# Down projection of an MLP as seven block products on one Trainium2 core, with the sums of weights on GpSimd

## The chip, the core and the metric

The kernel runs on one core of a Trainium2 chip. The core has TensorE (PE, matrix products into PSUM), VectorE (DVE), ScalarE (ACT), GpSimd (POOL) and SyncE (SP, which issues most DMAs). The metric is the time of one execution on the device in microseconds (us), as a median over runs.

## The reference

Two blocks follow one another on x of 512 positions by 1024 channels: a recurrent layer and an attention layer, then two hybrid layers. The change is in the MLP at the end of each hybrid layer:

```
h2 = rmsnorm(x, norm_mlp)
return x + jnp.square(jax.nn.relu(h2 @ w_up)) @ w_down     # w_up 1024x4096, w_down 4096x1024
...
for i in range(DEPTH):                                       # DEPTH = 2
    x = hybrid_layer(x, ...)
return rmsnorm(x, norm_final)
```

Everything is float32. On the chip each operand of a product is split into a high part (rounded to the matmul's input type) and a low part (the rest), and every product is three matmuls: high by high, high by low, low by high.

## The kernel before

**Layout.** Channels lie on the 128 partitions and positions on the free axis, so x is 8 tiles of 128x512. Weights come from HBM in chunks of 128x1024 (512 KB), each of which gives one output tile of 128 channels: 8 steps over the input channels, three matmuls each (`mm3`, L261 to L264).

**Stream of weights.** `Stream` loads the chunks in a fixed list `items` and splits each one: ACT writes the high part (L60), DVE subtracts to get the low part (L61). `next()` hands out one and emits the following one or two, so the weights of a pair are split while the pair before it is multiplied. Four raw buffers, three for high and three for low parts, and three for the split sums limit how far this runs ahead.

**MLP.** The 4096 hidden channels go in four groups of 1024 (`g`). In each group the up projection makes 8 hidden tiles, then the down projection adds their part to the 8 tiles of x. Up is done in *pairs* of output tiles by a Strassen-Winograd scheme: two output tiles by two halves of the positions are a 2x2 block product over two halves of the input channels, done in 7 block products instead of 8. Each block product is 4 steps of three matmuls with 256 columns, so 84 matmuls a pair. It needs sums of weight blocks S1 to S4 (`_emit_sums`, L63: two chunks come in, four adds of 128x512 on one engine, then two splits of 128x1024 and three of 128x512) and sums of x (T1 to T4, made once a layer by `PairNorm`). `W.pooled = 4` puts the adds of the first four pairs of a layer on POOL, the others on DVE. Each product has a PSUM bank of its own, and ACT, DVE and POOL combine the seven (L403 to L414). The hidden tile is then scaled by the row `r`, clipped at zero, squared and split (L1156, L1157, L277, L278).

**Down** is plain: per output tile 8 steps of three matmuls with 512 columns (192 matmuls in a group), then one DVE add into x (L1175). The last group of the last layer does three of its tiles by halves of the positions in `finish`, which also does the final norm and the output.

**Order.** PE's order is that of the code. On the other engines a scheduler orders the instructions at build time; each engine then runs its own list in that order and waits on semaphores, so whatever stands behind a waiting instruction waits too.

Of the kernel before, what the change touches and what calls it, by code (L numbers as in the profile page):

```python
# [7 lines left out]
F32 = mybir.dt.float32  # L8
# [40 lines left out]
class Stream:  # L49


    def __init__(self, tc, raw, hi, lo, items, ahead):
        self.nc, self.raw, self.hi, self.lo = tc.nc, raw, hi, lo
        self.items, self.ahead = items, ahead
        self.done, self.taken = [], 0
        self.sums = self.sraw = None
        self.pooled = 0
# [5 lines left out]
    def _emit_sums(self, i, s1, s2):  # L63
# [5 lines left out]
        eng = nc.gpsimd if self.pooled > 0 else nc.vector  # L69
        self.pooled -= 1  # L70
# [15 lines left out]
        def half(nm, src):  # L86
            h = self.sums.tile([P, nh], F32R, tag="shi", name=f"sh{i}{nm}")
            l = self.sums.tile([P, nh], F32R, tag="slo", name=f"sl{i}{nm}")
            self._split(h, l, src)
            out[nm] = tuple(t.rearrange("p (a b) -> p a b", b=P) for t in (h, l))  # L90
# [18 lines left out]
    def _emit(self):  # L109
        nc = self.nc  # L110
        src, a, b = self.items[len(self.done)]
        if a is None:
            return self._emit_sums(len(self.done), src, b)
# [19 lines left out]
    def next(self):  # L133
        ahead = 1 if self.items[self.taken][1] is None else self.ahead
        self.prefetch(self.taken + 1 + ahead)
        out = self.done[self.taken]
        self.done[self.taken] = None
        self.taken += 1
        return out

# [12 lines left out]
def build(tc, A, out, dbg=None):  # L153
# [3 lines left out]
    with ctx:  # L157
# [50 lines left out]
        for l in range(2):  # L208
# [21 lines left out]
            for g in range(4):  # L230
                for f in range(0, 8, 2):
                    items.append((A[f"w_up{l}"][8 * g + f], None, A[f"w_up{l}"][8 * g + f + 1]))
                for j in range(8):
                    add(f"w_down{l}", 8 * g + j, KD, P)
# [19 lines left out]
        xH = big.tile([P, KD, S], F32R, name="xH")  # L254
        xL = big.tile([P, KD, S], F32R, name="xL")
# [5 lines left out]
        def mm3(ps, wH, wL, aH, aL, start, stop):  # L261
            pe.matmul(ps, wH, aH, start=start, stop=False)  # L262
            pe.matmul(ps, wH, aL, start=False, stop=False)  # L263
            pe.matmul(ps, wL, aH, start=False, stop=stop)  # L264

        def proj(ps, wch, srcH=None, srcL=None, mid={}):
            h, l = wch
            srcH = xH if srcH is None else srcH
            srcL = xL if srcL is None else srcL
            for k in range(KD):  # L270
                mm3(ps, h[:, k], l[:, k], srcH[:, k], srcL[:, k], k == 0, k == KD - 1)
# [33 lines left out]
        class Norm:  # L305
# [8 lines left out]
            def split(self, j):  # L314
                g = self.gain[:, j:j + 1]
                act.activation(xH[:, j], x[:, j], AF.Copy, scale=g)
                self.last = dve.scalar_tensor_tensor(xL[:, j], x[:, j], g, xH[:, j].bitcast(F32), ALU.mult, ALU.subtract).ins
# [28 lines left out]
        class PairNorm:  # L346


            def __init__(self, tag, tp, gain, TH, TL):
                self.n = Norm(tag, tp)  # L350
                self.gain, self.TH, self.TL, self.tp, self.tag = gain, TH, TL, tp, tag
                self.rows = self.n.rows

            def tile(self, j):
                self.n.tile(j)
                if j < 4:
# [4 lines left out]
                    split(xH[:, j, :S2], xL[:, j, :S2], xa[:, :S2])  # L361
# [10 lines left out]
                split(xH[:, j], xL[:, j], xb)  # L372
                split(self.TH[:, k, 2:], self.TL[:, k, 2:], d[:, 2:])

        def pair(tag, forms, cp, cs, first=False):
# [3 lines left out]
            ps = {}  # L379

            def prod(n, wn, xn, ks=range(4), stop=True):
                if n not in ps:
                    ps[n] = psum(f"{tag}_{n}")[:, :S2]
                h, l = w[wn]
                for k in ks:
                    bh, bl = forms[xn](k)
                    mm3(ps[n], h[:, k], l[:, k], bh, bl, k == 0, stop and k == 3)

            steps = ((1, "A11", "B11"), (2, "A12", "B21"), (5, "S1", "T1"), (6, "S2", "T2"))
            if first:  # L390
                for st in steps:
                    prod(*st, range(3), False)
                for st in steps:
                    prod(*st, range(3, 4))
            else:
                for st in steps:
                    prod(*st)
            s1 = cs.tile([P, S2], F32, tag="s1", name=f"s1_{tag}")
            s5 = cs.tile([P, S2], F32, tag="s5", name=f"s5_{tag}")
            z = cs.tile([P, S2], F32, tag="sz", name=f"sz_{tag}")  # L400
            c1 = cp.tile([P, S], F32, tag="c", name=f"c1_{tag}")
            c2 = cp.tile([P, S], F32, tag="c", name=f"c2_{tag}")
            act.copy(s1, ps[1])  # L403
            dve.tensor_add(c1[:, :S2], ps[2], s1)
            act.copy(s5, ps[5])
            dve.tensor_add(z, ps[6], s1)  # L406
            pool.tensor_add(s5, s5, z)  # L407
            prod(7, "S3", "T3")
            dve.tensor_add(z, ps[7], z)
            dve.tensor_add(c2[:, S2:], ps[7], s5)  # L410
            prod(3, "S4", "B22")
            dve.tensor_add(c1[:, S2:], ps[3], s5)
            prod(4, "A22", "T4")
            dve.tensor_add(c2[:, :S2], ps[4], z)  # L414
            return c1, c2

        def x_forms(TH, TL):
            S2 = S // 2
            f = {f"T{i + 1}": (lambda k, i=i: (TH[:, k, i], TL[:, k, i])) for i in range(4)}
            f["B11"] = lambda k: (xH[:, k, :S2], xL[:, k, :S2])  # L420
            f["B21"] = lambda k: (xH[:, 4 + k, :S2], xL[:, 4 + k, :S2])
            f["B22"] = lambda k: (xH[:, 4 + k, S2:], xL[:, 4 + k, S2:])
# [209 lines left out]
        with ExitStack() as lc:  # L632
# [58 lines left out]
            def fox_v(c, mid=None):  # L691
# [4 lines left out]
                for tb in range(4):  # L696
                    ps = psum(f"v{c}_{tb}")[:, :n]
                    cs = slice(tb * P, (tb + 1) * P)
                    for k in range(KD):
                        h, l = w[k // kt]  # L700
                        mm3(ps, xH[:, k, cs], xL[:, k, cs], h[:, k % kt], l[:, k % kt], k == 0, k == KD - 1)
# [167 lines left out]
        def finish(ah, nrm, tp):  # L869

            S2, JS = S // 2, (5, 6, 7)
            ws = [W.next() for _ in JS]
            onesf = ones.bitcast(F32)
            for j in range(3, 5):
# [3 lines left out]
            def down(b, j, mid):  # L878
                h, l = ws[j - JS[0]]
                hs = slice(b * S2, (b + 1) * S2)  # L880
                ps = psum(f"dl{j}_{b}")[:, :S2]
                for k in range(8):
                    mm3(ps, h[:, k], l[:, k], ah[k][0][:, hs], ah[k][1][:, hs], k == 0, k == 7)
                    if k in mid:
                        mid[k]()
# [3 lines left out]
                if j == 7:  # L889
# [11 lines left out]
            def norm(b):  # L901
# [4 lines left out]
                for i, j in enumerate((3, 0, 1, 2, 4, 5, 6, 7)):  # L906
                    o = os[j // 4][:, j % 4 * S2:j % 4 * S2 + S2]
                    if j in (3, 4):
# [9 lines left out]

            none = {}
            down(0, 5, none)  # L920
            down(0, 6, none)
            down(0, 7, none)
            down(1, 5, {3: lambda: (sum_start(0), sum_end(0), norm(0))})
            down(1, 6, none)
            down(1, 7, none)
# [4 lines left out]
        for li in range(2):  # L930
# [3 lines left out]
            with ExitStack() as lc:  # L934
# [71 lines left out]
                for h in range(RET_H):  # L1006
# [13 lines left out]
                    for tb in range(4):  # L1020
                        ps = psum(f"rv{li}_{h}_{tb}")[:, :256]
                        cs = slice(tb * P, (tb + 1) * P)
                        for k in range(KD):
                            wh, wl = (h0, l0) if k < 4 else (h1, l1)
                            mm3(ps, xH[:, k, cs], xL[:, k, cs], wh[:, k % 4], wl[:, k % 4], k == 0, k == KD - 1)
# [56 lines left out]
            with ExitStack() as lc:  # L1082
# [50 lines left out]
                W.pooled = 4  # L1133
# [6 lines left out]
            with ExitStack() as lc:  # L1140
                t1 = lc.enter_context(tc.tile_pool(name=f"u{li}_1", bufs=1))
                t2 = lc.enter_context(tc.tile_pool(name=f"u{li}_2", bufs=2))
                t4 = lc.enter_context(tc.tile_pool(name=f"u{li}_4", bufs=4))
                ta = lc.enter_context(tc.tile_pool(name=f"u{li}_a", bufs=8))
                forms = x_forms(TH, TL)
                tn = Map(cs_h=(ta, "aH"), cs_l=(ta, "aL"), rs_m=(t4, "c"), rs_t=(t4, "c"), nsq=(t4, "c"))
                for g in range(4):
                    ah = []
                    for f in range(0, 8, 2):
                        cc = pair(f"up{li}_{g}_{f}", forms, t4, t2, g == 0 and f == 0)  # L1150
                        if g == 0 and f == 0:
                            r = nrm.rows(tn)
                            nrm = Norm(f"x{li}", tn, None if last else v("nmix1", 0, 8))
                        for i in range(2):
                            t = cc[i]
                            dve.scalar_tensor_tensor(t, t, 0.0, r, ALU.max, ALU.mult)  # L1156
                            act.activation(t, t, AF.Square)  # L1157
                            aH = ta.tile([P, S], F32R, tag="aH", name=f"aH{li}_{g}_{f + i}")
                            aL = ta.tile([P, S], F32R, tag="aL", name=f"aL{li}_{g}_{f + i}")
                            split(aH, aL, t)  # L1160
                            ah.append((aH, aL))
                    head = [(W.next(), psum(f"dn{li}_{g}_{j}")) for j in range(2)]
                    for ks in (range(6), range(6, 8)):
                        for (h, l), ps in head:
                            for k in ks:
                                mm3(ps, h[:, k], l[:, k], ah[k][0], ah[k][1], k == 0, k == 7)
                    for j in range(5 if last and g == 3 else 8):
                        if j < 2:
                            ps = head[j][1]
                        else:  # L1170
                            h, l = W.next()
                            ps = psum(f"dn{li}_{g}_{j}")
                            for k in range(8):
                                mm3(ps, h[:, k], l[:, k], ah[k][0], ah[k][1], k == 0, k == 7)
# [113 lines left out]
```

## Time and profile before

| | |
|---|---|
| median of 3 runs | 2275.84 us (2275.23 to 2277.53) |
| the profiled execution | 2277.16 us, of which the span from first to last instruction is 2275.1 us |
| PE busy | 98% of the span |
| DVE, ACT, POOL busy | 68%, 47%, 16% |
| granted TensorE clock, mean | 0.989 of full speed |

The profiled execution lies 1.3 us above the median. An engine counts as busy also while an instruction that it has begun is held up inside the engine, so a busy share is no measure of work done. DVE pipelines: the next instruction begins about 0.08 us before the one ahead of it ends, so the step from start to start is what an instruction costs.

### The profile page before, as it was taken

Reading aid. Unit: us, or ns where it says so; the run is one execution under the profiler, and the core shown is the slowest. Engines: PE = TensorE matmul, PEld = TensorE weight load, DVE = VectorE, ACT = ScalarE, POOL = GpSimd, SP = SyncE. Lnnn points to the kernel's source line nnn. Section 1 sums busy time; section 2 is a strip of 40 time slices with the busy share of each in tenths; the row PEclk is TensorE's granted clock in tenths of the full one; section 3 lists DMA queues with packets and bytes.
Section 4 is the critical chain, followed back from the end, with each engine's and each line's share of the span. In section 5 each row is a group of like instructions: output and inputs, shape, how many; then the busy total and the mean of one; then the engine's idle time right before and its main releaser. Section 6 shows DMA issues by size and latency. Waiting matters only on the chain.

```text
span 2275.1 us, 30068 instructions
## 1 busy us (share of the span) xinstructions
PE 2220.2 (98%) x11818; PEld 1912.8 (84%) x11818; DVE 1543.0 (68%) x2256; ACT 1066.3 (47%) x1629; POOL 372.7 (16%) x269
## 2 busy tenths in 40 slices
PE   8899999999999999999999999999999999999998
PEld 6687778887888888887998998988888887998997
DVE  8988877777776445448876785676345448886774
ACT  5666577765555222235543444556222235543443
POOL 3435211113211000003310112211000003310112
PEclk9999999999999999999999999999999999999999
DMA  4123222122232322222332333222332232333231
GB/s 155 64 95 102 90 66 75 65 74 81 71 105 75 100 95 95 100 93 84 104 101 95 110 103 102 90 92 74 102 102 93 97 98 76 110 103 101 96 110 56
DMA packets 62509, 210.42 MB, mean 92 GB/s; under 512 B 6944, under 2 KB 11424, under 8 KB 62368
## 3 DMA queue, kind: packets, MB, share of 16 engines
q1 hardware_dynamic: 59552, 204.43, 27.2%
q10 hardware_dynamic: 2672, 3.81, 0.5%
q8 instruction: 93, 1.52, 0.3%
q14 instruction: 48, 0.39, 0.1%
q0 software_dynamic: 144, 0.26, 0.0%
HBM read 206.37 MB, written 2.10 MB: 92 GB/s over the span
## 4 chain that ended last, share of the span: by engine, by line
PE 83%; DVE 4%; ACT 1%; issue 1%; POOL 0%; DVEq 0%; ACTq 0%; POOLq 0%
PE dn L263 5%; PE dn L262 5%; PE dn L264 5%; PE up L263 5%; PE up L264 5%; PE up L262 5%; PE ro L987 1%; PE gb L262 1%; PE cu L263 1%; PE cc L263 1%; PE cb L263 1%; PE wr L263 1%; PE gb L263 1%; PE gb L264 1%; PE wc L262 1%
## 5 line engine op out<-in xcount | busy, mean ns | idle before, releaser
L60 ACT CAST wh<-wr 128x1024 fp32r<-128x1024 f32 (+2 forms) x332 | 337.5, 1018 | 691.0 <-PE dn L263 110.1
L61 DVE TENSOR_TENSOR wl<-wr,wh 128x1024 fp32r<-128x1024 f32 (+2 forms) x332 | 401.0, 1209 | 49.4 <-ACT wh L60 47.2
L263 PE MATMUL dn<-aL,wh 128*128 128x512 f32 x488 | 190.0, 389 | 0.0
L262 PE MATMUL dn<-aH,wh 128*128 128x512 f32 x488 | 190.0, 389 | 0.0
L264 PE MATMUL dn<-aH,wl 128*128 128x512 f32 x488 | 189.9, 389 | 0.0
L407 POOL TENSOR_TENSOR s_up<-s_up,sz_up 128x256 f32<-128x256 f32 x32 | 52.6, 1644 | 465.8 <-DVE sz_up L406 163.8
L1175 DVE TENSOR_TENSOR x<-dn,x 128x512 f32<-128x512 f32 x61 | 42.0, 688 | 102.2 <-PE dn L264 102.2
L263 PEld LDWEIGHTS dn<-aL,wh 128*128 128x128 f32 x488 | 91.6, 188 | 19.1 <-DVE aL L278 0.5
L264 PEld LDWEIGHTS dn<-aH,wl 128*128 128x128 f32 x488 | 91.6, 188 | 19.1
L262 PEld LDWEIGHTS dn<-aH,wh 128*128 128x128 f32 x488 | 91.6, 188 | 18.9
L334 POOL TENSOR_TENSOR nacc_m<-nacc_m,nsq_m 128x512 f32<-128x512 f32 x14 | 21.0, 1497 | 482.7 <-ACT nsq_m L333 482.7
L264 PE MATMUL rv<-wh,xL 128*128 128x256 f32 x256 | 72.5, 283 | 0.0
L263 PE MATMUL rv<-wl,xH 128*128 128x256 f32 x256 | 72.5, 283 | 0.0
L262 PE MATMUL rv<-wh,xH 128*128 128x256 f32 x256 | 72.4, 283 | 0.0
L1157 ACT ACTIVATE c_up<-c_up 128x512 f32<-128x512 f32 x64 | 40.5, 633 | 34.7 <-DVE c_up L1156 33.5
L262 PE MATMUL rg<-xH,wh 128*128 128x512 f32 x128 | 49.9, 390 | 0.0
L262 PE MATMUL gb<-xH,wh 128*128 128x512 f32 x128 | 49.9, 390 | 0.0
L264 PE MATMUL rg<-xH,wl 128*128 128x512 f32 x128 | 49.8, 389 | 0.0
L263 PE MATMUL rg<-xL,wh 128*128 128x512 f32 x128 | 49.8, 389 | 0.0
L264 PE MATMUL gb<-xH,wl 128*128 128x512 f32 x128 | 49.8, 389 | 0.0
L263 PE MATMUL gb<-xL,wh 128*128 128x512 f32 x128 | 49.8, 389 | 0.0
L262 PE MATMUL wr<-yrH,wh 128*128 128x512 f32 x128 | 49.8, 389 | 0.0
(1561 smaller groups left out, 7146.3 us busy)
## 6 DMA issues: line engine op xcount, KB each, us to landing
wr<-in_w_in SPq DMA_DIRECT2D x112, 512.0 KB, 3.5
wr<-in_w_down SPq DMA_DIRECT2D x64, 512.0 KB, 3.5
wr<-in_fox_w_in SPq DMA_DIRECT2D x24, 512.0 KB, 3.5
wr<-in_lru_w_in SPq DMA_DIRECT2D x23, 512.0 KB, 3.6
wr<-in_w_v SPq DMA_DIRECT2D x16, 512.0 KB, 3.4
wr<-in_w_ret_out SPq DMA_DIRECT2D x16, 512.0 KB, 3.5
wr<-in_w_conv_out SPq DMA_DIRECT2D x16, 512.0 KB, 3.4
wr<-in_w_o SPq DMA_DIRECT2D x16, 512.0 KB, 3.5
```

What stands on the lines that cost most here:

```text
L60: self.nc.scalar.copy(h, src)
L61: self.nc.vector.tensor_sub(l, src, h.bitcast(F32))
L262: pe.matmul(ps, wH, aH, start=start, stop=False)
L263: pe.matmul(ps, wH, aL, start=False, stop=False)
L264: pe.matmul(ps, wL, aH, start=False, stop=stop)
L334: (dve if j > 5 and acc is self.acc2 else pool).tensor_add(acc, acc, sq)
L407: pool.tensor_add(s5, s5, z)
L987: pe.matmul(po[i][:, q0:], vp[:, kb, vs], sp_[:, so], start=n == 0, stop=n == 11)
L1157: act.activation(t, t, AF.Square)
L1175: dve.tensor_add(x[:, j], ps, x[:, j])
```

## The change

The down projection is done by the same seven products as up, on pairs of output tiles. For this the hidden tiles are written as blocks and sums of blocks (B11, B21, B22, T1 to T4) while up is finished, so up now pairs the hidden tiles k and k+4 of a group. A pair uses three PSUM banks instead of seven: bank `h6` gets S2·T2, DVE adds the first product to it in PSUM (L446), and later products accumulate on top (`start=False`). ACT copies intermediate states out (`s1`, `z`, `s5`, `u3`), with one set of four buffers for all pairs. All sums of weights go to POOL, except one of the four (S3) for down pairs, which is DVE's (`mine`). In groups 0 to 2 POOL also adds parts of the down result into x. Tiles are placed anew so that all fits, which moves no work elsewhere in the program. The last pairs in `finish` follow the same scheme.

```diff
-    def _emit_sums(self, i, s1, s2):
+    def _emit_sums(self, i, s1, s2, mine):
-        eng = nc.gpsimd if self.pooled > 0 else nc.vector
-        self.pooled -= 1
+        eng, eng3 = nc.gpsimd, nc.vector if mine else nc.gpsimd
...
         v1 = sraw("S1")
         eng.tensor_add(v1, a21, a22)
         half("S1", v1)
-        eng.tensor_sub(a21, a11, a21)
-        whole(("S3", "A22"), r2)
         v2 = sraw("S2")
         eng.tensor_sub(v2, v1, a11)
         half("S2", v2)
+        eng3.tensor_sub(a21, a11, a21)
+        whole(("S3", "A22"), r2)
         v4 = sraw("S4")
         eng.tensor_sub(v4, a12, v2)
         half("S4", v4)
...
-                for j in range(8):
-                    add(f"w_down{l}", 8 * g + j, KD, P)
+                for j in range(0, 8, 2):
+                    items.append((A[f"w_down{l}"][8 * g + j], None, (A[f"w_down{l}"][8 * g + j + 1], True)))
...
+        def product(w, forms, ps, wn, xn, new, ks=range(4)):
+            h, l = w[wn]
+            for k in ks:
+                bh, bl = forms[xn](k)
+                mm3(ps, h[:, k], l[:, k], bh, bl, new and k == 0, k == 3, not new)
...
+            h1, h6, h5 = (psum(f"{tag}_{n}")[:, :S2] for n in (1, 6, 5))
...
+            steps = ((h1, "A11", "B11"), (h6, "S2", "T2"), (h5, "S1", "T1"))
...
+            s1, z, s5, u3 = scratch(tag)
+            act.copy(s1, h1)
+            dve.tensor_add(h6, h6, s1)
+            act.copy(z, h6)
+            act.copy(s5, h5)
+            prod(h1, "A12", "B21", False)
+            yield 11, h1, ()
+            prod(h6, "S3", "T3", False)
+            act.copy(u3, h6)
+            yield 22, None, (u3, s5)
+            prod(h5, "S4", "B22", False)
+            yield 12, h5, (z,)
+            prod(h6, "A22", "T4", False)
+            yield 21, h6, ()
...
+                def up(g, k):
...
+                        if n == 22:
+                            pool.tensor_add(t, *more)
+                            dve.tensor_mul(t, t, r[:, hs])
+                            act.activation(t, t, AF.Relu)
+                        else:
+                            for m in more:
+                                dve.tensor_add(ps, ps, m)
+                            dve.scalar_tensor_tensor(t, ps, 0.0, r[:, hs], ALU.max, ALU.mult)
+                        act.activation(t, t, AF.Square)
+                        if n == 11:
+                            split(B1[0][:, k], B1[1][:, k], t)
+                        elif n == 12:
+                            dve.tensor_sub(d[:, 0], at[12], at[11])
+                            dve.tensor_sub(d[:, 1], at[22], d[:, 0])
+                            split(TA[0][:, k, :2], TA[1][:, k, :2], d[:, :2])
+                            dve.tensor_sub(d[:, 2], at[22], at[12])
+                    d = mlp.d
+                    split(B2[0][:, k], B2[1][:, k], ta2)
+                    dve.tensor_sub(d[:, 3], at[21], d[:, 1])
+                    split(TA[0][:, k, 2:], TA[1][:, k, 2:], d[:, 2:])
+
+                def down(g, j):
+                    xs = {11: x[:, j, :S2], 12: x[:, j, S2:], 21: x[:, j + 1, :S2], 22: x[:, j + 1, S2:]}
+                    for n, ps, more in pair(f"dn{li}_{g}_{j}", aforms, scratch, j == 0):
+                        for m in more:
+                            (dve if g == 3 else pool).tensor_add(xs[n], xs[n], m)
+                        if ps is not None:
+                            dve.tensor_add(xs[n], ps, xs[n])
```

POOL's list in the up projection of group 1 of the first hybrid layer (`s_up` and `sz_up` are combined products, `sr` raw sums of weights, `wr` raw chunks, `t` a hidden tile, `free` the four buffers); before, the eight pairs of groups 1 and 2:

```order
L407 TENSOR_TENSOR s_up_1_0_9933<-s_up_1_0_9933,sz_up_1_0_9934 128x256
L407 TENSOR_TENSOR s_up_1_2_10081<-s_up_1_2_10081,sz_up_1_2_10082 128x256
L407 TENSOR_TENSOR s_up_1_4_10229<-s_up_1_4_10229,sz_up_1_4_10230 128x256
L407 TENSOR_TENSOR s_up_1_6_10352<-s_up_1_6_10352,sz_up_1_6_10353 128x256
L407 TENSOR_TENSOR s_up_2_0_10781<-s_up_2_0_10781,sz_up_2_0_10782 128x256
L407 TENSOR_TENSOR s_up_2_2_10929<-s_up_2_2_10929,sz_up_2_2_10930 128x256
L407 TENSOR_TENSOR s_up_2_4_11077<-s_up_2_4_11077,sz_up_2_4_11078 128x256
L407 TENSOR_TENSOR s_up_2_6_11200<-s_up_2_6_11200,sz_up_2_6_11201 128x256
```

and with the change, the sums for two pairs:

```order
L98 TENSOR_TENSOR sr187S_10251<-wr187b 128x512
L103 TENSOR_TENSOR wr187b<-wr187a,wr187b 128x512
L1249 TENSOR_TENSOR t_0_9008<-free_9064 128x256
L101 TENSOR_TENSOR sr187S_10257<-sr187S_10251,wr187a 128x512
L106 TENSOR_TENSOR sr187S_10268<-wr187a,sr187S_10257 128x512
L1249 TENSOR_TENSOR t_0_9008<-free_9064 128x256
L98 TENSOR_TENSOR sr188S_10397<-wr188b 128x512
L103 TENSOR_TENSOR wr188b<-wr188a,wr188b 128x512
L101 TENSOR_TENSOR sr188S_10403<-sr188S_10397,wr188a 128x512
L106 TENSOR_TENSOR sr188S_10414<-wr188a,sr188S_10403 128x512
```

Where POOL had one add of 128x256 for each pair it now has that and four adds of 128x512.

DVE's list for an up pair of group 2, first hybrid layer, before (`c_up` is a hidden tile in the making, `wl` and `sl` low parts of weights and of sums):

```order
L61 TENSOR_TENSOR wl203A_10850<-wr203a,wh203A_10849 128x1024
L1156 SCALAR_TENSOR_TENSOR c_up_2_0_10784<-c_up_2_0_10784,r_m_9126 128x512
L404 TENSOR_TENSOR c_up_2_2_10931<-up_2_2_2_10889,s_up_2_2_10928 128x256
L278 TENSOR_TENSOR aL_2_0_10836<-c_up_2_0_10783,aH_2_0_10835 128x512
L61 TENSOR_TENSOR wl203S_10861<-wr203b,wh203S_10860 128x1024
L61 TENSOR_TENSOR sl203S_10856<-sr203S_10853,sh203S_10855 128x512
L406 TENSOR_TENSOR sz_up_2_2_10930<-up_2_2_6_10915,s_up_2_2_10928 128x256
L61 TENSOR_TENSOR sl203S_10867<-sr203S_10864,sh203S_10866 128x512
L278 TENSOR_TENSOR aL_2_1_10842<-c_up_2_0_10784,aH_2_1_10841 128x512
L105 TENSOR_TENSOR sr203S_10870<-wr203a,sr203S_10864 128x512
```

and with the change (`up_2_0_1`, `_6`, `_5` are the PSUM banks h1, h6, h5; `A` the blocks of hidden tiles, `tmp` and `t` raw hidden tiles, `d` their differences):

```order
L446 TENSOR_TENSOR up_2_0_6_11229<-up_2_0_6_11229,free_9064 128x256
L61 TENSOR_TENSOR sl194S_11208<-sr194S_11205,sh194S_11207 128x512
L61 TENSOR_TENSOR sl194S_11214<-sr194S_11211,sh194S_11213 128x512
L1255 SCALAR_TENSOR_TENSOR tmp_r_9081<-up_2_0_1_11228,r_m_9055 128x256
L61 TENSOR_TENSOR wl194S_11219<-wr194b,wh194S_11218 128x1024
L317 TENSOR_TENSOR A_9007<-tmp_r_9081,A_9007 128x256
L1254 TENSOR_TENSOR up_2_0_5_11230<-up_2_0_5_11230,free_9064 128x256
L1255 SCALAR_TENSOR_TENSOR tmp_r_9081<-up_2_0_5_11230,r_m_9055 128x256
L61 TENSOR_TENSOR sl194S_11225<-sr194S_11222,sh194S_11224 128x512
L1250 TENSOR_TENSOR t_0_9008<-t_0_9008,r_m_9055 128x256
L1255 SCALAR_TENSOR_TENSOR t_0_9008<-up_2_0_6_11229,r_m_9055 128x256
L1260 TENSOR_TENSOR d_9063<-tmp_r_9081 128x256
```

The adds of weights are gone from DVE's list; many small instructions on halves of hidden tiles have come in, and the next weights' splits stand between them.

DVE's list for the start of the down projection of group 2, before:

```order
L278 TENSOR_TENSOR aL_2_7_11261<-c_up_2_6_11203,aH_2_7_11260 128x512
L1175 TENSOR_TENSOR x<-dn_2_0_11276,x 128x512
L61 TENSOR_TENSOR wl_11279<-wr_11277,wh_11278 128x1024
L1175 TENSOR_TENSOR x<-dn_2_1_11283,x 128x512
L61 TENSOR_TENSOR wl_11336<-wr_11334,wh_11335 128x1024
L1175 TENSOR_TENSOR x<-dn_2_2_11340,x 128x512
```

and with the change, one pair:

```order
L446 TENSOR_TENSOR dn_2_0_6_11813<-dn_2_0_6_11813,free_9064 128x256
L61 TENSOR_TENSOR sl198S_11792<-sr198S_11789,sh198S_11791 128x512
L61 TENSOR_TENSOR sl198S_11798<-sr198S_11795,sh198S_11797 128x512
L1275 TENSOR_TENSOR x<-dn_2_0_1_11812,x 128x256
L61 TENSOR_TENSOR wl198S_11803<-wr198b,wh198S_11802 128x1024
L103 TENSOR_TENSOR wr199b<-wr199a,wr199b 128x512
L1275 TENSOR_TENSOR x<-dn_2_0_5_11814,x 128x256
L61 TENSOR_TENSOR sl198S_11809<-sr198S_11806,sh198S_11808 128x512
L1275 TENSOR_TENSOR x<-dn_2_0_6_11813,x 128x256
L61 TENSOR_TENSOR wl199A_11915<-wr199a,wh199A_11914 128x1024
```

Two splits and two adds for two tiles have become ten instructions for two tiles.

## Rows read from the trace of the kernel before

**Rows 1.** The page: span, busy time by engine, and the chain by engine.

```profile
span 2275.1 us, 30068 instructions
PE 2220.2 (98%) x11818; PEld 1912.8 (84%) x11818; DVE 1543.0 (68%) x2256; ACT 1066.3 (47%) x1629; POOL 372.7 (16%) x269
...
PE 83%; DVE 4%; ACT 1%; issue 1%; POOL 0%; DVEq 0%; ACTq 0%; POOLq 0%
```

**Rows 2.** Busy us (instructions) by stretch: an up, then a down projection.

```profile
core 0: us, PE busy (x) PEld busy (x) DVE busy (x) ACT busy (x) POOL busy (x), PEclk, DMA share, GB/s
...
1161.00:1200.80 39.80, 39.80 (x337) 39.80 (x336) 36.17 (x62) 23.15 (x37) 7.23 (x4) 1.00 0.33 106
1200.80:1244.60 43.80, 43.80 (x196) 36.28 (x196) 23.39 (x31) 12.90 (x16) 0.00 (x0) 1.00 0.29 97
```

**Rows 3.** Timeline of PE: first matmul of each half of group 1.

```profile
1160.98 0.28 PE L262 MATMUL up<-xH,wh189A 128*128 128x256 f32 x1
...
1200.87 0.40 PE L262 MATMUL dn<-aH,wh 128*128 128x512 f32 x1
...
1244.43 0.28 PE L262 MATMUL up<-xH,wh201A 128*128 128x256 f32 x1
```

**Rows 4.** Timeline of DVE while POOL rests (start, us, instruction).

```profile
1171.78 0.68 DVE L1156 SCALAR_TENSOR_TENSOR c_up<-c_up,r_m 128x512 f32<-128x512 f32 x1
1172.38 0.41 DVE L414 TENSOR_TENSOR c_up<-up,sz_up 128x256 f32<-128x256 f32 x1
1172.72 0.68 DVE L102 TENSOR_TENSOR sr191S<-sr191S,wr191a 128x512 f32<-128x512 f32 x1
1173.32 1.21 DVE L61 TENSOR_TENSOR wl191A<-wr191a,wh191A 128x1024 fp32r<-128x1024 f32 x1
1174.45 0.68 DVE L1156 SCALAR_TENSOR_TENSOR c_up<-c_up,r_m 128x512 f32<-128x512 f32 x1
```

**Rows 5.** Timeline of DVE while POOL works, before the first up pair.

```profile
1066.00 1.51 DVE L370 TENSOR_TENSOR d_m<-xgb_m,xga_m 128x256 f32<-128x256 f32 x1
1067.43 1.51 DVE L371 TENSOR_TENSOR d_m<-xgb_m,d_m 128x256 f32<-128x256 f32 x1
1068.86 1.78 DVE L278 TENSOR_TENSOR xL<-xgb_m,xH 128x512 fp32r<-128x512 f32 x1
```

**Rows 6.** Timeline of POOL in the same stretch.

```profile
1065.75 1.47 POOL L334 TENSOR_TENSOR nacc_m<-nacc_m,nsq_m 128x512 f32<-128x512 f32 x1
1067.18 1.47 POOL L99 TENSOR_TENSOR wr178b<-wr178a,wr178b 128x512 f32<-128x512 f32 x1
1068.62 1.47 POOL L102 TENSOR_TENSOR sr178S<-sr178S,wr178a 128x512 f32<-128x512 f32 x1
```

**Rows 7.** Timeline of POOL in the up projection of group 0.

```profile
1094.57 1.30 POOL L105 TENSOR_TENSOR sr179S<-wr179a,sr179S 128x512 f32<-128x512 f32 x1 [3.03 <-DVE sl179S L61]
1095.82 1.19 POOL L407 TENSOR_TENSOR s_up<-s_up,sz_up 128x256 f32<-128x256 f32 x1
```

**Rows 8.** Timeline of DVE in the same stretch.

```profile
1094.68 1.73 DVE L61 TENSOR_TENSOR sl179S<-sr179S,sh179S 128x512 fp32r<-128x512 f32 x1
1096.34 1.22 DVE L293 SCALAR_TENSOR_TENSOR r_m<-rst_m,r_m 128x512 f32<-128x512 f32 x1
```

**Rows 9.** Busy time around it, columns as in rows 2.

```profile
1084.00:1101.00 17.00, 17.00 (x144) 16.92 (x142) 17.00 (x21) 8.83 (x13) 13.24 (x9) 1.00 0.35 121
```

**Rows 10.** POOL's adds by line: ns min/median/max.

```profile
L105 POOL TENSOR_TENSOR sr180S<-wr180a,sr180S x1: 1298/1298/1298, 1108.3 to 1108.3; 128x512 f32<-128x512 f32 x1
...
L892 POOL TENSOR_TENSOR nacc_x<-nacc_x,lsq x4: 723/736/802, 2248.8 to 2263.2; 128x256 f32<-128x256 f32 x4
```

**Rows 11.** Busy time where PE waits on splits, columns as in rows 2.

```profile
1060.00:1084.00 24.00, 19.20 (x101) 16.72 (x100) 22.74 (x29) 15.32 (x26) 10.68 (x8) 0.86 0.21 69
```

More of the change, by code (lines that the diff above doesn't have):

```diff
@@ L139, in next, with __init__, tile @@
         return out
+class Fixed:
+    def __init__(self, **m):
+        self.m, self.n = m, {}
+    def tile(self, shape, dtype, tag, name):
+        n = self.n[tag] = self.n.get(tag, -1) + 1
+        t = self.m[tag][n % len(self.m[tag])][:, :shape[-1]]
+        return t if dtype == t.dtype else t.bitcast(dtype)
 class Map:
@@ L377, in pair @@
+        def pair(tag, forms, scratch, late=False):
             w = W.next()
             S2 = S // 2
[L379 to L389, printed above, removed]
@@ L917, in norm @@
                         )
[L919 to L925, printed above, removed]
+            late = []
+            for j in (4, 6):
+                w = W.next()
+                h1, h6, h5 = (psum(f"dl{j}_{n}")[:, :S2] for n in (1, 6, 5))
+                s1, z, s5, u3 = scratch(j)
+                product(w, forms, h1, "A11", "B11", True)
+                product(w, forms, h6, "S2", "T2", True)
+                act.copy(s1, h1)
+                dve.tensor_add(h6, h6, s1)
+                act.copy(z, h6)
+                product(w, forms, h1, "A12", "B21", False)
+                block(0, j, h1)
+                product(w, forms, h6, "S3", "T3", False)
+                act.copy(u3, h6)
+                dve.tensor_add(x[:, j, S2:], x[:, j, S2:], z)
+                dve.tensor_add(x[:, j + 1, S2:], x[:, j + 1, S2:], u3)
+                product(w, forms, h6, "A22", "T4", False)
+                block(0, j + 1, h6, last=j == 6)
+                late.append((j, w, h5))
+            for j, w, h5 in late:
+                product(w, forms, h5, "S1", "T1", True)
+                block(1, j + 1, h5)
+                if j == 6:
+                    sum_start(0)
+                    sum_end(0)
+                    norm(0)
+            for j, w, h5 in late:
+                product(w, forms, h5, "S4", "B22", False)
+                block(1, j, h5, last=j == 6)
             sum_start(1)
@@ L1140, in build @@
             with ExitStack() as lc:
[L1141 to L1144, printed above, removed]
-                forms = x_forms(TH, TL)
-                tn = Map(cs_h=(ta, "aH"), cs_l=(ta, "aL"), rs_m=(t4, "c"), rs_t=(t4, "c"), nsq=(t4, "c"))
-                for g in range(4):
[L1148 to L1174, printed above, removed]
-                        dve.tensor_add(x[:, j], ps, x[:, j])
@@ new lines, in build, with scratch, first_rows @@
+                tmp = {}
+                class mlp:
+                    free = None
+                def scratch(tag):
+                    if not mlp.free:
+                        first_rows()
+                        mlp.d, mlp.free = quarters(0, f"d{li}"), quarters(1, f"free{li}")
+                    return [mlp.free[:, i] for i in range(4)]
+                def first_rows():
+                    cs = xs.lend(0, F32R, f"mcs{li}")
+                    rs = xs.lend(1, F32, f"mrs{li}")
+                    mlp.r = nrm.rows(Fixed(cs_h=[cs[:, 0]], cs_l=[cs[:, 1]], rs_m=[rs[:, 0]], rs_t=[rs[:, 1]]))
```

163 lines of the change are left out of this document (101 added, 62 removed).

## The prediction

> **What bounds the kernel now.** I began with the page. PE is busy for 98% of the span and the chain that ended last runs through PE for 83% of it; DVE has 68%, POOL 16% [rows 1]. So far this says only that PE is the bound on average. The second view is the busy time by stretch for one group of the MLP: in the up half PE is busy 39.80 of 39.80 us, in the down half 43.80 of 43.80, at the full clock (PEclk 1.00) [rows 2]. PE never waits there, so fewer columns on PE would shorten the time one for one, as long as the others keep up. The same rows show how near the others are: DVE is busy 36.17 of 39.80 us in up and only 23.39 of 43.80 in down. Down is where DVE makes good what it fell behind in up.
>
> The third view is the timeline of DVE and POOL, for what their instructions cost alone and beside each other. Alone, DVE steps 0.60 us for 512 elements a partition, 0.34 for 256 and 1.13 for 1024 [rows 4]; POOL needs 1.30 us for an add of 512 and 0.72 for 256 [rows 10]. Beside each other it is different. Where POOL adds without a pause, DVE's subtractions of 256 step 1.43 us (1066.00, 1067.43, 1068.86) [rows 5], and POOL's adds of 512 step 1.43 and 1.44 (1065.75, 1067.18, 1068.62) [rows 6]. Both engines have one step of 1.43, four times DVE's own 0.34: they take turns, one DVE instruction, one POOL instruction. With DVE's turn at 0.34, POOL's turn for 512 is 1.43 - 0.34 = 1.09 us. For 256, an instruction of DVE that needs 0.68 lasts 1.22 when an add of 256 is just ahead of it (1095.82 on POOL, 1096.34 on DVE) [rows 7, 8], so that turn is 0.54. DVE instructions that read PSUM don't take part: in the stretch of rows 9 those on `up` tiles stay at 0.41. What takes part are the ones with both inputs in SBUF: all splits, differences, sums and multiplications by `r` of tiles in SBUF.
>
> That stretch of 17.0 us [rows 9] also says how full the turns get when both have work enough. Its timeline holds, on POOL, six adds of 512, two of 256 and 0.5 us of one begun before: 6.54 + 1.08 + 0.5 = 8.1 us of turns; on DVE ten instructions of 512 and two of 1024 with both inputs in SBUF: 6.0 + 2.26 = 8.3 us. Together 16.4 of 17.0, or 96%. It is one resource, and it was full. PE didn't notice, since only a layer's first pairs have their sums on POOL, and the down half follows.
>
> **What PE gains.** A down half has 192 matmuls of 512 columns from 1200.87 to 1244.43, 43.56 us; an up half has 336 of 256 columns from 1160.98 to 1200.87, 39.89 us [rows 3]. Down by seven products has the same 336, so a group falls from 83.45 to 79.78 us: 3.67 less. Seven groups give 25.7 us. In the last one, before has 120 matmuls at 43.56/192 = 0.227 us and 144 of 256 columns at 39.89/336 = 0.119, 44.4 us, against 39.9: 4.5 less. If PE stays the bound this is 30.2 us.
>
> **What the others get to do**, in turns of the shared resource. *Up pair.* DVE: two splits of 1024 and three of 512 for weights (2.26 + 1.80), one of 256 and three of 512 for hidden tiles (0.34 + 1.80), one multiplication by `r` and four differences of 256 (1.70): 7.90 us. POOL: four sums (4.36) and one add of 256 (0.54): 4.90. Together 12.80 us, where PE needs 9.97. Before, with the sums on DVE, POOL had only the add of 256. *Down pair.* DVE: 4.06 for the weights, 0.60 for S3: 4.66. POOL: three sums (3.27) and three adds of 256 (1.62): 4.89. Together 9.55, against 9.97. DVE's instructions on PSUM (five in an up pair, four in a down pair, 0.34 each) come under POOL's turns at best, as most did in rows 9.
>
> So the up half no longer fits. At the 96% of rows 9 an up pair takes 12.80 / 0.96 = 13.33 us and a down pair 9.55 / 0.96 = 9.95, which is PE's own 9.97. Down is then as full as up used to be, and nothing is made good there. Nor may DVE lag: the product S3·T3 accumulates onto `h6` only after DVE has added the first product to it (L446) and ACT has copied the sum out (`z`). Between the end of S2·T2 and S3·T3 PE has two products, 2.85 us, and L446 stands in DVE's list behind the last differences and splits of the pair before. If DVE is later than about 2 us (2.85 less the add and the copy), PE waits within the pair, and all that is queued behind on PE too. Before, the seven banks were read by nobody on whom PE depended so soon.
>
> **Sum.** A group takes 4 x 13.33 + 4 x 9.97 = 93.2 us instead of 83.45: 9.75 more. Eight groups: 78.0. In the last group of the last layer the time before is 39.9 + 44.4 = 84.3, so 0.8 comes off. In group 0 of each layer the sums of the first pair are made during the output projection ahead of it, as before, and the excess of one pair falls away: 3.4 us, twice. 78.0 - 0.8 - 6.8 = 70.4, on 2277.2 of the profiled execution 2347.6, and with the 1.3 us by which that lies above the median, **2346 us**.
>
> **Bounds.** The turns can be smaller than DVE's steps, since the next instruction begins 0.07 to 0.08 us before the one ahead ends (0.68 long, 0.60 from start to start [rows 4]). With DVE at 0.53, 0.27 and 1.06 us, POOL's turn is 1.43 - 0.27 = 1.16. An up pair is then 6.9 + 5.2 = 12.1 and a down pair 4.2 + 5.1 = 9.3; with every turn used, and down making good what up lost, a group takes 85.7, 2.2 above before: 8 x 2.2 - 0.8 = 17, or 2293 us. On the other side, if none of DVE's PSUM instructions falls under a turn of POOL, a pair takes 12.80 + 1.70 = 14.5 and 9.55 + 1.36 = 10.9 us, a group 101.6: 18.2 more, eight times, less 0.8: 2421 us. I take the value between, from the stretch that is nearest: same engines, same kinds of instruction, both with work waiting.
>
> Rows 5 and 6 give a turn that is shorter than the instruction. The Trainium skill ("SBUF — State Buffer", section "Who interferes with whom") says that a VectorE instruction with two inputs in SBUF and a GpSimd one that reads SBUF exclude each other, and that the second blocks until the first is through with its whole instruction. The trace agrees that they exclude each other (1.43 = 0.34 + 1.09). It doesn't agree on the length: taken at its word, POOL's 1.30 and 0.72 us would be its turns, an up pair 13.8, a down pair 10.7 and the kernel about 2393 us.
>
> What costs nothing: the DMAs (the same chunks, two at once for down; the DMA share is 0.29 to 0.33 [rows 2]); ACT (each down pair gains casts and copies, about 2.7 us beside 12.90 busy of 43.80; up gains about 2 us a pair beside 23.15 of 39.80), though ACT's copies wait for DVE. PE's clock fell to 0.86 in the stretch where it waited on splits [rows 11]; idle PE has time to spare, so I count nothing.
>
> **Rivals.**
> 1. *PE stays the bound: faster.* If one pair's turns overlap more than I think, so that a group's work on DVE and POOL fits in PE's 79.8 us, the 30.2 us come out whole: 2245.6 us. For it: in DVE's own steps up is 9.6 us a pair (7.90 + 1.70), less than 9.97, and POOL's is 4.9. Against it: rows 5, 6 and 9. It decides below 79.8 us of turns for a group; mine come to 85.7 at the very least.
> 2. *More than the turns: about 2421 us or more.* DVE, ACT and POOL wait for each other in order (a sum on POOL, its cast on ACT, its split on DVE, then the PE product), and with one set of four buffers those waits leave turns unused. For it: the turns in rows 9 were full only because both had a backlog. Against it: DVE and POOL have work of the next pair in hand most of the time.
> 3. *No change: about 2276.* Waits of 3.7 us a group, just what PE gains. For it only that rows 2 show DVE close to full before and PE without a wait.
>
> **Chances.** My forecast 0.74, with a range of its own from 2293 to 2400; rival 1 0.13; rival 2 0.10; rival 3 0.03. Executions agree within about 0.2%, so that less can't be told from no change. Faster 0.13, same 0.03, slower 0.84. The range from 2293 to 2405 leaves out rival 1 and most of rival 2.
>
> **What the profile after would show.** PE's busy time some 30 us smaller but its share near 93%; PE waiting in the up halves on DVE's splits, or on ACT's copy `z` and through it on L446, a few us a pair, and hardly in the down halves; up halves of about 53 us, down halves of about 40; DVE's differences in up at 1.0 us and more instead of 0.41, splits of 512 well above 0.68, instructions on PSUM still 0.41; POOL's busy time about twice what it was. I am wrong if DVE's splits keep their 0.68 us beside POOL's adds, if PE shows no wait in up, or if the waits are on POOL or ACT with DVE idle.

## The result and the profile after

The changed kernel takes 2409.91 us (median of 4 runs, 2408.12 to 2411.84) beside 2276.69 for the kernel before: a ratio of 1.0582, 95% interval 1.0563 to 1.0600, or 133 us more. The direction is the predicted one; the size is nearly twice the forecast's 70 us, and the time lies 5 us above the top of the range (2405).

The page of the profiled execution, to be read beside [rows 1]:

```profile
span 2406.4 us, 33510 instructions
...
PE 2241.4 (93%) x12898; PEld 1971.1 (82%) x12898; DVE 1782.9 (74%) x2501; ACT 1223.1 (51%) x2076; POOL 743.7 (31%) x534
...
PE 60%; DVE 21%; POOL 4%; issue 4%; ACT 2%; DVEq 0%; ACTq 0%; POOLq 0%
```

The span grew by 131.3 us. PE's busy time grew by 21.2, its idle time (span less busy) from 54.9 to 165.0, by 110.1. DVE and POOL now hold 25% of the chain.

Busy time of the stretches of the first hybrid layer, columns as in [rows 2]: groups 0 and 1 (up, down, up, down), and the down half of group 3.

```profile
1067.96:1129.71 61.75, 45.68 (x340) 43.18 (x338) 55.95 (x80) 38.95 (x77) 26.39 (x19) 0.86 0.22 69
1129.71:1178.91 49.20, 42.81 (x339) 41.91 (x337) 41.85 (x53) 25.68 (x47) 31.25 (x26) 0.93 0.25 82
1178.90:1228.94 50.04, 43.36 (x338) 41.79 (x337) 48.17 (x66) 30.91 (x65) 32.76 (x21) 0.97 0.26 89
1228.94:1275.86 46.92, 41.60 (x338) 40.93 (x337) 39.58 (x52) 24.34 (x44) 30.16 (x23) 0.93 0.26 85
...
1423.68:1476.55 52.87, 43.82 (x339) 42.48 (x338) 49.97 (x70) 29.72 (x55) 20.66 (x13) 0.90 0.26 87
```

Where [rows 2] had 39.80 and 43.80 us with PE always busy, group 1 now has 50.04 and 46.92, and PE waits in both. Group 2 is like it (49.4 and 48.3). Group 0 (61.75 and 49.20) and the down half of group 3 (52.87) are worse.

The timeline of PE at the edges of group 1's down half, against [rows 3]:

```profile
1228.94 0.28 PE L302 MATMUL dn<-A,wh189A 128*128 128x256 f32 x1
...
1237.86 0.58 PE L302 MATMUL dn<-A,sh189S 128*128 128x256 f32 x1 [5.18 <-ACT A L316]
...
1246.24 0.28 PE L302 MATMUL dn<-A,wh190A 128*128 128x256 f32 x1
...
1275.86 0.29 PE L302 MATMUL up<-xHa,wh193A 128*128 128x256 f32 x1
```

The first down pair lasts 17.30 us (1228.94 to 1246.24), of which 5.18 are one wait; the other three take 29.62 together, 9.87 each, which is PE's own pace. So the loss of a down half is in its first pair. What PE waits for there is ACT's rounding of the last hidden tile (L316), which comes after DVE's differences of it.

PE's longest waits over the whole program (total us, times, longest):

```profile
PE dn L302 <- ACT A L316: 40.8, 8, 5.2
PE up L302 <- ACT free L445: 25.6, 11, 6.3
PE up L302 <- ACT free L447: 21.1, 19, 2.1
PE psr L303 <- DVE xcL L574: 8.4, 3, 3.3
PE up L302 <- ACT TH L316: 6.6, 2, 3.3
```

The first row is that edge, once in each of the 8 groups. L445 and L447 are ACT's copies `s1` and `z` of the seven products. The wait on `xcL` stood with the same 8.4 us in the kernel before and belongs to another stage.

DVE's timeline of group 1:

```profile
1183.16 0.42 DVE L446 TENSOR_TENSOR up<-up,free 128x256 f32<-128x256 f32 x1
...
1202.73 1.51 DVE L317 TENSOR_TENSOR A<-tmp_nacc,A 128x256 fp32r<-128x256 f32 x1
1204.17 1.51 DVE L1250 TENSOR_TENSOR t<-t,r_m 128x256 f32<-128x256 f32 x1
1205.60 0.42 DVE L1254 TENSOR_TENSOR up<-up,free 128x256 f32<-128x256 f32 x1
...
1221.98 0.42 DVE L446 TENSOR_TENSOR up<-up,free 128x256 f32<-128x256 f32 x1
...
1233.65 1.89 DVE L61 TENSOR_TENSOR wl190A<-wr190a,wh190A 128x1024 fp32r<-128x1024 f32 x1
...
1237.84 1.30 DVE L317 TENSOR_TENSOR A<-d,A 128x512 fp32r<-128x512 f32 x2 [0.23 <-ACT A L316]
1239.41 0.43 DVE L446 TENSOR_TENSOR dn<-dn,free 128x256 f32<-128x256 f32 x1 [0.28 <-PE dn L304]
...
1250.10 0.42 DVE L446 TENSOR_TENSOR dn<-dn,free 128x256 f32<-128x256 f32 x1
```

The turns of [rows 5] are back: 1.51 us for 256 elements with both inputs in SBUF, 0.42 with one in PSUM. L446 stands once in each pair and so marks DVE's pace: three up pairs from 1183.16 to 1221.98, 12.94 us each; then 17.43 across the edge from up to down. DVE ends its work on the last hidden tile at 1239.14, 10.2 us after PE has ended the up half, and a split for a later pair (`wl190A`) stands ahead of it in the list. In the kernel before this was 5.1 us (1205.96 against 1200.87):

```profile
1205.27 0.69 DVE L278 TENSOR_TENSOR aL<-c_up,aH 128x512 fp32r<-128x512 f32 x1 [0.75 <-ACT aH L277]
```

POOL in the changed kernel, in group 1's up half, where adds of 512, 1.30 us alone [rows 10], last longer:

```profile
1201.69 2.27 POOL L98 TENSOR_TENSOR sr188S<-wr188b 128x512 f32<-128x512 f32 x1
1204.04 1.36 POOL L103 TENSOR_TENSOR wr188b<-wr188a,wr188b 128x512 f32<-128x512 f32 x1
```

### The profile page after: what moved, and what is told of

Same layout as the page of the kernel before. It is cut to its first block, busy times and chain, and to the rows that moved or that the text cites. A ratio compares the mean times of both kernels' runs of the same rounds, so it can differ in the third digit from the quotient of the medians.

```text
span 2406.4 us, 33510 instructions
## 1 busy us (share of the span) xinstructions
PE 2241.4 (93%) x12898; PEld 1971.1 (82%) x12898; DVE 1782.9 (74%) x2501; ACT 1223.1 (51%) x2076; POOL 743.7 (31%) x534
## 4 chain that ended last, share of the span: by engine, by line
PE 60%; DVE 21%; POOL 4%; issue 4%; ACT 2%; DVEq 0%; ACTq 0%; POOLq 0%
DVE A L317 3%; PE dn L303 2%; PE dn L304 2%; PE dn L302 2%; PE ro L1048 1%; PE gb L302 1%; PE gb L303 1%; PE wc L304 1%; PE ga L304 1%; PE cu L302 1%; PE cc L302 1%; PE cb L302 1%; PE wr L302 1%; PE ga L302 1%; PE cu L304 1%
## 5 line engine op out<-in xcount | busy, mean ns | idle before, releaser
L60 ACT CAST wh<-wr 128x1024 fp32r<-128x1024 f32 (+1 forms) x268 | 270.0, 1009 | 529.2 <-issue 72.9
L61 DVE TENSOR_TENSOR wl<-wr,wh 128x1024 fp32r<-128x1024 f32 (+1 forms) x268 | 323.5, 1209 | 45.6 <-ACT wh L60 43.7
L1273 POOL TENSOR_TENSOR x<-x,free 128x256 f32<-128x256 f32 x72 | 79.0, 1098 | 27.3 <-ACT free L447 23.4
L1014 POOL TENSOR_TENSOR rarq<-rarq,rbrq 128x512 f32<-128x512 f32 x8 | 17.5, 2193 | 142.8 <-DVE rbrq L1013 142.8
L316 ACT CAST A<-d 128x512 fp32r<-128x512 f32 x64 | 39.0, 621 | 39.5 <-DVE d L1261 29.8
L317 DVE TENSOR_TENSOR A<-d,A 128x512 fp32r<-128x512 f32 x64 | 56.6, 902 | 1.8 <-ACT A L316 1.8
L303 PE MATMUL rv<-wl,xHa 128*128 128x256 f32 x192 | 54.3, 283 | 0.0
L304 PE MATMUL rv<-wh,xLa 128*128 128x256 f32 x192 | 54.3, 283 | 0.0
L302 PE MATMUL rv<-wh,xHa 128*128 128x256 f32 x192 | 54.3, 283 | 0.0
L303 PE MATMUL wr<-yrL,wh 128*128 128x512 f32 x128 | 49.8, 389 | 0.0
L304 PE MATMUL wr<-yrH,wl 128*128 128x512 f32 x128 | 49.8, 389 | 0.0
L302 PE MATMUL wc<-zH,wh 128*128 128x512 f32 x128 | 49.8, 389 | 0.0
```

Source lines behind the costliest of these rows:

```text
L60: self.nc.scalar.copy(h, src)
L61: self.nc.vector.tensor_sub(l, src, h.bitcast(F32))
L302: pe.matmul(ps, wH, aH, start=start, stop=False, skip_group_check=more)
L303: pe.matmul(ps, wH, aL, start=False, stop=False, skip_group_check=more)
L304: pe.matmul(ps, wL, aH, start=False, stop=stop, skip_group_check=more)
L316: act.copy(dH, src)
```

## The experiments

My theory: the sums on GpSimd cost what they cost because POOL's reads of SBUF and DVE's instructions with both inputs there take turns, and DVE has no slack left. The main rival: it is the order of waits and the chains through three banks that cost, whoever reads what.

**The turns alone.** The kernel before, with a test behind the last output: ten adds of 128x512 on DVE beside ten instructions on POOL, three times.

```diff
...
+for n in range(3):
+    dve.tensor_add(db, db, gc)
+    pool.tensor_add(gb, gb, db)
+    for i in range(10):
+        dve.tensor_add(dc, bps if n == 1 else da, db)
+        if n == 2:
+            pool.memset(gc, 1.0)
+        else:
+            pool.tensor_add(gc, ga, gb)
```

> The kernel before with three short stretches behind its last output: ten adds of 512 on DVE beside ten on POOL; DVE with both inputs in SBUF beside POOL adds, then one input in PSUM beside POOL adds, then both in SBUF beside POOL fills. Theory of turns: in the first stretch both step about 0.6 + 1.1 = 1.7 us; in the second and third DVE steps about 0.6 and POOL as it does alone, 1.25 for adds. Rival (POOL and DVE share bandwidth, whatever they read): slower steps in all three.

DVE's timeline (a row stands for all ten):

```profile
2279.03 15.70 DVE L1194 TENSOR_TENSOR bt<-bt 128x512 f32<-128x512 f32 x10
...
2297.95 7.22 DVE L1194 TENSOR_TENSOR bt<-b_ps,bt 128x512 f32<-128x512 f32 x10
...
2313.44 8.17 DVE L1194 TENSOR_TENSOR bt<-bt 128x512 f32<-128x512 f32 x10
```

and POOL's:

```profile
2280.92 16.27 POOL L1198 TENSOR_TENSOR bt<-bt 128x512 f32<-128x512 f32 x10
...
2299.34 13.34 POOL L1198 TENSOR_TENSOR bt<-bt 128x512 f32<-128x512 f32 x10
2313.48 1.77 POOL L1192 TENSOR_TENSOR bt<-bt,bt 128x512 f32<-128x512 f32 x1 [0.81 <-DVE bt L1191]
2315.19 5.76 POOL L1196 MEMSET bt<- 128x512 f32 x10
```

With both inputs in SBUF the engines share one step, 1.67 us from start to start on both. (Over all ten it is 1.57 and 1.63, because DVE's first add, 0.69, runs before POOL's begin and POOL's last, 1.26, after DVE's have ended.) With one DVE input in PSUM each goes at its own step, 0.72 and 1.33; 0.60 and 1.25 were expected. Beside fills, which read nothing, DVE needs 8.17, which is 7.22 and one turn of 0.95 for the single add (L1192) ahead of the fills. So the turns are real, they need both engines to read SBUF, and a pair of 512 and 512 costs 1.67 us; the prediction's terms give 0.60 + 1.09 = 1.69.

**POOL's sums without reads.** In the changed kernel each sum on POOL becomes two fills of the same tile.

```diff
+        def fill(t):
+            for _ in range(2):
+                nc.gpsimd.memset(t, 0.01)
-        eng.tensor_add(v1, a21, a22)
+        fill(v1)
...
-        eng3.tensor_sub(a21, a11, a21)
+        eng3.tensor_sub(a21, a11, a21) if mine else fill(a21)
```

> The changed kernel with each sum of weights on POOL replaced by two fills of the same tile on POOL, which read nothing from SBUF (so the weights' sums are wrong, and POOL's part of them has the same place in the order). Theory of turns (POOL's reads and DVE's two-input instructions exclude each other, which stretches DVE's work on an up pair from 9.6 to about 14 us): DVE is back at its own steps, 0.68 for 512 and 0.41 for 256, PE's waits in up all but go, 2255 to 2300 us. Rival of order (PE now waits in each pair for DVE's L446 and ACT's copies, and at the turn from up to down for the last hidden tiles; POOL is not the cause): the waits stay, 2370 us or more.

It measured 2292.29 us, 1.0059 of before (1.0044 to 1.0074), 117.6 less than the changed kernel. Its rows on DVE in group 1 (count | busy us, mean ns | idle; line numbers are four higher in the two runs with fills) have the uncontended durations of [rows 4]:

```profile
L1254 DVE TENSOR_TENSOR t<-t,r_m 128x256 f32<-128x256 f32 x5 | 2.1, 413 | 0.0
...
L61 DVE TENSOR_TENSOR sl188S<-sr188S,sh188S 128x512 fp32r<-128x512 f32 x3 | 2.0, 678 | 0.0
```

Up halves of groups 1 to 3 are back at 39.9 us, PE's pace; down halves are at 44.4 to 45.9. The chains through ACT, DVE and three banks, for which PE waits, are still there, so the rival, which wanted 2370 or more, falls. A fill does wait for less than a sum, since it reads neither a chunk nor another sum. But it wasn't late sums that held up DVE in the changed kernel: in group 1's up half DVE was busy for 48.17 of 50.04 us, and its instructions had got longer. What stays is the wait at the edge, shorter:

```profile
PE dn L306 <- ACT A L320: 22.8, 8, 2.9
PE up L306 <- ACT free L449: 9.5, 2, 4.9
```

**The same sums in the kernel before.** All 16 up pairs of a layer have their sums on POOL, and down stays plain (edit to the kernel before):

```diff
-                W.pooled = 4
+                W.pooled = 16
```

> The kernel before with the sums of all 16 up pairs of a layer on POOL instead of the first four: the part of the change on GpSimd alone. Theory of turns: DVE falls some 5 us further behind in each up half, and the plain down half, where DVE works 23 of 44 us, takes that up, as it does now in group 0: 2276 to 2300 us. If the sums on POOL cost by themselves, wherever they stand: 2330 us or more.

It measured 2276.80 us, 0.9997 of before (0.9987 to 1.0006). Its up half of group 1:

```profile
1158.46:1198.35 39.89, 39.89 (x338) 39.89 (x336) 37.35 (x50) 22.20 (x37) 16.53 (x12) 1.00 0.28 93
```

PE doesn't wait at all. The sum of turns says why. POOL's timeline of this stretch has nine adds of 512 and three of 256, 9.81 + 1.62 = 11.4 us of turns; DVE's has 21 instructions of 512 and 8 of 1024 with both inputs in SBUF, 12.6 + 9.0 = 21.6. Together that is 33.1 of 39.9 us: it fits, since only nine of a half's sixteen sums are made here (the others in the plain down half ahead) and hidden tiles need fewer instructions. DVE ends the last hidden tile 6.6 us after PE has ended up, and the down half has its 43.56 us all the same. The same sums cost nothing here, and a good deal where down has no slack (next runs).

**Who does the sums.** All of them on DVE, or those of up pairs alone:

```diff
-        eng, eng3 = nc.gpsimd, nc.vector if mine else nc.gpsimd
+        eng = eng3 = nc.vector
```

> The changed kernel with all sums of weights on DVE, up's and down's: the down projection by seven products without the part on GpSimd. Theory of turns: an up pair as with up's sums on DVE alone (12.5 us), a down pair 4.66 + 1.80 + 1.36 of DVE and 1.62 of POOL, 9.4, less than PE's 9.97; the sums of the first down pairs, which fall into up, get cheaper too: 2340 to 2366 us, a little below the 2367 with up's sums on DVE. If POOL relieved DVE in the down halves: 2375 us or more.

```diff
-        eng, eng3 = nc.gpsimd, nc.vector if mine else nc.gpsimd
+        eng, eng3 = nc.gpsimd if mine else nc.vector, nc.vector
```

> The changed kernel with the four sums of an up pair back on DVE, those of a down pair as they are. Theory of turns: on DVE a sum of 512 costs 0.60 us of the shared resource, on POOL 1.09; an up pair takes DVE 7.9 + 2.4 + 1.7 us of steps and 0.5 of POOL's add, 12.5, instead of about 14: 8 x 4 x 1.5 = 48 us less, 2340 to 2385 us. Rival (DVE's list is what is too long, and POOL relieved it): 2.4 us a pair more, 2440 us or more.

All on DVE: 2349.65 us, 1.0311 (1.0294 to 1.0328). Up's alone: 2367.19 us, 1.0391 (1.0376 to 1.0407). So giving the sums to GpSimd costs 60.3 us against leaving them on DVE: 42.7 for up's, 17.5 for down's. But down by seven products without it is already some 72 us slower than before. In group 1 its up half lasts 44.1 us and its down half 47.9, where 39.9 and 39.2 are PE's pace. In that up half DVE is busy for 42.69 of 44.12 us, POOL for 4.86: DVE alone has too much to do.

**The edge.** The first down pair of each group reads hidden tile 0 where it should read tile 3 (all forms but B11), so that it need not wait for the last one.

```diff
+                eforms = {n: (f if n == "B11" else lambda k, f=f: f(k % 3)) for n, f in aforms.items()}
...
-                    for n, ps, more in pair(f"dn{li}_{g}_{j}", aforms, scratch, j == 0):
+                    for n, ps, more in pair(f"dn{li}_{g}_{j}", eforms if j == 0 else aforms, scratch, j == 0):
```

> The changed kernel, but the first down pair of each group reads hidden tile 0 in place of hidden tile 3 in all forms except B11 (wrong data, same work), so that it doesn't wait for the last up pair. Theory of turns: DVE is behind by its whole list, L446 of that pair stands behind the same work, and the wait of 5.2 us moves to a later product: 2390 to 2410 us. Rival of order: the wait is one of latency at the edge, and eight waits of 5.2 us and the slower clock after them go: 2350 to 2370 us.

It measured 2398.00 us, 1.0525 (1.0507 to 1.0542): 12 us less, though 40.8 us of waits on L316 are gone. They moved:

```profile
PE dn L302 <- ACT free L447: 29.5, 20, 3.6
```

DVE is behind by then, so PE waits for the next thing that comes through DVE, the copy `z` after L446. Group 1 still takes 96.9 us: from the fourth up pair on, L446 steps 13.50 and 13.60 us with DVE never at rest, where the changed kernel has 17.43 and 10.69. The edge is where the lag shows, not what makes it. With the fills as well:

> Both edits at once: POOL's sums replaced by fills, and the first down pair of a group reading hidden tile 0 in place of 3 (both give wrong data, with the same work on PE). With the fills alone PE waited only at the turns from up to down (22.8 us in eight waits, and a slower clock after each) and 9.5 us in the layers' first pairs. Theory of turns: without POOL's reads DVE keeps up, so here the edge is a matter of latency, and taking it away leaves PE as the bound but for the first pairs: 2250 to 2268 us. If DVE is still behind without POOL's reads, the waits move on, as they did with the edge alone: 2280 us or more.

This measured 2264.17 us, 0.9940 (0.9925 to 0.9955). Without the turns the same edit is worth 28 us, and down halves fall to about 41 (43.2 in group 3). PE's longest waits in the MLP are then these, and the line of its page gives its busy time:

```profile
PE dn L306 <- ACT free L451: 12.0, 10, 1.3
PE up L306 <- ACT free L449: 9.6, 2, 4.9
```

```profile
PE 2188.3 (97%) x12898; PEld 1936.8 (86%) x12898; DVE 1612.5 (71%) x2501; ACT 1226.4 (54%) x2076; POOL 594.5 (26%) x758
```

PE's busy time is 31.9 us below that of the kernel before, and its idle time 22.0 above (76.9 against 54.9). So this run lies 18.6 us above the 2245.6 of rival 1 by waits. Those of L451 are new; up had 9.5 us of waits before too, there for splits of x.

**POOL's adds into x.** All of them on DVE, as in group 3.

```diff
-                            (dve if g == 3 else pool).tensor_add(xs[n], xs[n], m)
+                            dve.tensor_add(xs[n], xs[n], m)
```

> The changed kernel with the adds into x of groups 0 to 2 on DVE instead of POOL (nine adds of 256 for three down pairs). The down pairs after a group's first one ran at PE's own pace, 9.8 us: with 1.0 us more for DVE and 1.6 less for POOL's turns they stay there: 2395 to 2415 us, no more than 0.6% from the changed kernel. If POOL's adds into x had a part in the loss: 2390 us or less; if DVE's list were the limit in down: 2425 us or more.

It measured 2406.02 us, 1.0559 (1.0543 to 1.0575): 4 us less than the changed kernel, with intervals that overlap. These adds are at most a small part of the cost.

## Why the prediction was right in direction and too small

- **PE's gain** was sized right: where nothing holds PE, a down pair takes 9.80 us (9.97 forecast), and in the fastest variant, 2264 us, PE is busy for 31.9 us less than before (30.2 forecast). Of these that variant loses 18.6 again to waits.
- **The turns** were right. The test shows them (1.67 us for 1.69), and the fills take 117.6 of the 133 us away. In up DVE's pace came out at 12.94 us a pair against 13.33, with turns for 92% of the time (in the three pairs shown, 16 instructions of 512, 6 of 1024 and 14 of 256 on DVE, 21.1 us, and 12 adds of 512 and 3 of 256 on POOL, 14.7, in 38.8), and instructions on PSUM kept 0.42. What is full is DVE's list, not POOL's: POOL waits for splits in between, as it did for 3.03 us in the stretch of rows 9 [rows 7], where I took both to have a backlog. So many instructions meet no turn: of DVE's 72 differences in the up halves of groups 1 to 3, 54 last about 0.41, though I had named 1.0 and more as a sign.
- **The bound from whole instructions** (2393 us) is nearer the measured time than the sum, but by luck: by whole instructions the step in the test would be about 0.7 + 1.3 = 2.0 us, and 1.67 was measured. The Trainium skill ("SBUF — State Buffer", "Who interferes with whom") says that a VectorE instruction with two inputs in SBUF doesn't contend with a GpSimd instruction which only writes. The fills agree (5.76 us for ten, with one turn in all on DVE, that of the add ahead).
- **The step that failed** is the sum over pairs: "Down is then as full as up used to be, and nothing is made good there", with waits "hardly in the down halves". I took four up pairs and four down pairs, each at the longer of PE and turns, and let PE pay each pair's excess where it arises. In fact PE runs ahead in up (pairs of 11.2, 11.4, 13.6 and 13.9 us in group 1: 50.0, not 53.3), and DVE's lag is paid in the first down pair, which reads the last hidden tile: 17.3 us instead of 9.97. Group 1 takes 97.0 us and group 2 97.7, not 93.2. I had looked for a reader soon after DVE only within a pair (L446), not across the edge. The lag has grown from 5.1 to 10.2 us, and it is due sooner. The kernel before does steps 0 to 5, of eight over the hidden tiles, for both of its first two down tiles before steps 6 and 7 of either, so PE came to the last two hidden tiles 8.2 us into down (1200.87 to 1209.07). Now it wants the last one 3.7 us in (1228.94 to 1232.68). That the read itself isn't the whole of it, the run on the edge shows: without it DVE's work on the last hidden tile still runs on into the first two down pairs.
- **Where the miss lies**: the span missed by 61 us, of which some 25 are in the two groups 0, 17 in the four groups 1 and 2, and 20 in the two groups 3 and what follows the last.
- **Group 0**: "the excess of one pair falls away" was wrong. Its first pair takes 27.1 us (18.2 before). ACT's copy `s1`, which PE needs after three products, stands behind the norm. ACT, then PE:

```profile
1087.12 0.37 ACT L445 COPY free<-up 128x256 f32<-128x256 f32 x1 [4.47 <-DVE r_m L332]
```

```profile
1087.54 0.58 PE L302 MATMUL up<-xHa,wh177A 128*128 128x256 f32 x1 [6.28 <-ACT free L445]
```

  With seven banks no product of a pair waited for a copy. The group takes 111.0 us, 19 more than before (91.9), where I counted 6.
- **Group 3** takes 102.9 us in the first layer instead of 83.4 + 9.75. Its down half also holds the next stage's splits of x, which lay in DVE's slack before (893 ns each) and now last longer, as DVE's instructions beside POOL's adds do (a line of DVE in that half: count | busy us, mean ns | idle):

```profile
L356 DVE SCALAR_TENSOR_TENSOR xLa<-x,vec,xHa 128x512 fp32r<-128x512 f32 x6 | 9.2, 1547 | 0.0
```

- **The clock**: "idle PE has time to spare, so I count nothing" left out a term. I had PE's busy time at 30 less and its idle time at 101 more; they came out at 21 more and 110 more, so of the 61 us by which the span missed 51 stand under busy. The 30 less was right where waits are few (2188.3 us above), so the rest goes with the waits. PE's timeline has some 200 matmuls in the first layer, 15 to 32 a half, with a step of 0.21 us instead of 0.12, right behind waits: about 19 us a layer. In the stretch behind the wait of 5.18 the granted clock (PEclk) is 0.50, the lower level:

```profile
1237.80:1240.80 3.00, 2.80 (x11) 2.51 (x12) 2.62 (x5) 2.05 (x6) 0.06 (x1) 0.50 0.00 0
```

  How much of it lengthens the program isn't settled: in up, where DVE is late anyway, a slower PE only waits less. No run took the clock apart from the waits.

Of the rivals, the first (PE stays the bound) and the third (no change) fell. The second, waits in order on top of the turns, priced at 2421 or more, is near the measured time. The edge and the first pair are waits of its sort, though not at the place I named (sum, cast, split); but its price came from up pairs of 14.5 us, and 12.94 were measured, so the nearness is luck.

No version here that computes the reference's result beats the kernel before. Even with fills in place of POOL's sums it is 0.6% slower, and with the edge gone as well only 0.6% faster.

## What to carry to other kernels

Before a stage with slack is made leaner, see whose lag that slack absorbed: here the plain down half took up GpSimd sums of up (which cost 43 us once it was gone) and the tail of the hidden tiles. Cost a periodic schedule from marks that recur on the late engine (L446 here) across its edges, not from the sum of its pairs; here the reader of the last hidden tile paid the lag. Where VectorE had no slack and its other instructions read two inputs from SBUF, an add moved from it to GpSimd freed nothing: 0.60 us saved, about 1 us of turns spent.

## What the runs showed of the hardware

Adds of 128x512 on VectorE and GpSimd, all inputs in SBUF, went at one common step of 1.67 us; with a VectorE input in PSUM at 0.72 and 1.33; and beside GpSimd fills VectorE wasn't slowed (8.17 us for ten, 0.95 of it the turn of an add). The turn of a GpSimd add, 0.95 to 1.09 us, was shorter than the 1.30 that it lasts alone. Behind a wait of 5.18 us in a stream of matmuls the granted clock was 0.50, and the first matmuls went at 0.21 us instead of 0.12.
